# GLA block on one core: the projections' stage reordered (operand turns, token sums, gate rows, decays, r's weights)

## The chip, the core and the metric

The kernel runs on one core of one Trainium2 chip. The metric is the device time of one execution in microseconds. A core has TensorE (PE; its weight loads are PEld), VectorE (DVE), ScalarE (ACT), GpSimd (POOL) and SyncE (SP), which issues nearly all DMAs here; all of them run on their own and meet at semaphores.

## What is computed

One decoder layer on 1024 tokens of width 1024, in float32: RMSNorm, gated linear attention, residual, RMSNorm, squared-ReLU MLP, residual, and a final RMSNorm. What matters here is the head of the mixer:

```python
proj = h @ w_in
q, k, v, r, gk_low = jnp.split(proj, ...)          # 512, 512, 1024, 1024, 16 columns
log_a = jax.nn.log_sigmoid(gk_low @ w_gk_up + b_gk) / 16
...                                                 # per chunk: cumulative sum b of log_a
o_inter = einsum(q * exp(b), state); attn = (q, k, decay by differences of b); k_dec = k * exp(b_last - b)
...
o = rms_norm(o, g_onorm); return (o * silu(r)) @ w_out
```

h is the normed x. The norm's per-token factor (rstd) isn't applied to x: the projections run on x times the norm's gain, and rstd is put in where it is used.

## The kernel before

**Products.** Large products are done in a fast 2 x 2 block form with seven block products instead of eight: each side has blocks "11", "12", "21", "22" of 512 x 512, and some of the seven operands are sums of blocks, built in place ("t" is a temporary). `form` (lines 142 to 148) lists, for the n-th product, the operand and the sums that it needs first. A side of one form sums n=1: t = 21 + 22; n=2: t = t - 11 and 21 = 11 - 21; n=3: t = 12 - t; the other form has t = 12 - 11, then t = 22 - t and 12 = 22 - 12, and for the last product t = 21 - t. A block product is one *step*: 4 lanes of 128 rows by 4 slices of k, and for each three matmuls of 128x128x512, since every operand is split into a high and a low part (`split`, lines 77 to 80: ACT copies to the rounded type, DVE subtracts). So a step has 48 matmuls and takes four splits of 128x1024, two for each side. Step (i, at) is the at-th step of chunk i; its n is taken from PLAIN = (0, 5, 1, 2, 3, 4, 6). Chunk 0 is Q and K (weights W as stationary side, x as moving side), chunk 1 is V (x stationary, weights moving).

**Order.** `chunks_of` (lines 241 to 279) walks the steps: it runs the hooks of step (i, at), asks for the next weights at steps 5 and 6, makes the operands of the *next* step (`operand`: sums and splits), and then issues the matmuls of this one. A hook with four numbers (i, at, lane, kp) runs inside the step, behind that lane's matmuls of that k slice; such a step goes lane by lane. PE's instructions keep the order of the source. Those of the other engines and of SP's DMA queue are ordered by a planner: each has the place in the source as its priority, evictions (lines 422 and 437) are raised, and the planner issues what it reckons ready. On the chip each engine then follows that fixed order.

**Buffers.** SBUF tiles come from tags with few buffers: "big" 8 (split operands, four for each step), "vx" 8 (x blocks, later v), "wa" 6 and "wb" 4 (weights and "t"), "raw" 2, "g4" 6, "hq" 4. PSUM has "gl" 5 and "mm" 3. A tile is taken when one of its tag is free.

**The stage.** Lines 338 to 376 load the first blocks of x and W, then the others, w_gk (the 16 gate columns) and w_up. Lines 379 to 388 split the gate weights. `gk_half` (line 391) computes 16 gate rows for half of the tokens in 16 matmuls on x's split operands: the first half ahead of step (0,1), the second ahead of step (0,5), on an x "12" split of its own (`x12_split`, line 730). `token_rms` (line 401) squares x row by row on ACT for rstd. Each x operand of chunk 0 but n = 0 and 5 is stored to DRAM (`xv`, line 311) and read back in chunk 1 by `KeptX` (line 443), which for n = 0 and 5 fetches x again and splits it. `spread_rms` (line 467) puts rstd into the gate rows. `prep_fast` (line 505) makes one head's gates and decays for half of the tokens, four for the first half in steps (1,0) and (1,1). `load_wr` (line 677) fetches and splits r's weights, eight pieces of 512 KB. Behind chunk 1 come, for each of eight token blocks, `r_part` (line 695, 48 matmuls in four parts), the state, the outputs, and `outputs_T` (line 663), which transposes the block's output; the last block's runs in a hook of the output projection's first step.

## Time and profile before

| | us |
|---|---|
| median of 3 runs (1053.05 to 1056.13) | 1053.35 |
| profiled execution, its own time | 1055.77 |
| its span | 1054.0 |
| PE busy | 1016.8 |
| DVE busy | 730.7 |
| ACT busy | 548.2 |
| mean granted clock of TensorE | 0.986 |

The profile is of one execution. Its views name an instruction by line, engine and operation, then "out<-in" by tile names without their numbers ("big<-wa" writes a split operand from a weight tile), and how many are merged (x16). In the timeline a bracket tells how long the engine stood before and what ended that. Durations of matmuls include the tail of the pipeline, so two rows can overlap. In a table of stretches each engine has its busy time and its number of instructions; then come the granted clock of TensorE (1.00 is full speed), the mean share of the DMA engines in use, and GB/s.

### The profile page before, as it was taken

How to read it: one execution, taken by the hardware profiler on the slowest of the kernel's cores; microseconds unless marked ns; L12 is line 12 of the kernel's file. 1: busy time of each engine (PE TensorE's matmuls, PEld its weight loads, DVE VectorE, ACT ScalarE, POOL GpSimd, SP SyncE). 2: the span in 40 equal slices, each digit the busy share in tenths (PEclk: the TensorE clock that was granted, in tenths of full speed). 3: DMA queues.
4: the chain of work that ended last, by engine and by line, in shares of the span. 5: the costliest groups of instructions: out<-in, count | busy, mean ns of one | idle time of the engine just before them, and what ended most of it. 6: DMA issues, size and time to landing. Idle time of an engine off the chain costs nothing.

```text
span 1054.0 us, 12272 instructions
## 1 busy us (share of the span) xinstructions
PE 1016.8 (96%) x4614; PEld 842.8 (80%) x4614; DVE 730.7 (69%) x910; ACT 548.2 (52%) x828; POOL 198.5 (19%) x114
## 2 busy tenths in 40 slices
PE   7889889999999999999999999999999999999996
PEld 6768668778888788888888888888888888888885
DVE  5975594567657897897987336986427975338975
ACT  6571664566657436866633345533347332547355
POOL 0000030100000000004224232404330404331361
PEclk9999899999999999999999999999999999999998
DMA  9779575432224421477122575033674043762004
GB/s 267 254 307 343 199 269 211 123 105 82 92 81 154 127 71 49 181 284 275 40 81 67 205 290 217 21 91 110 219 299 160 1 121 118 274 233 94 1 1 163
DMA packets 104340, 165.33 MB, mean 157 GB/s; under 512 B 5584, under 2 KB 75344, under 8 KB 94032
## 3 DMA queue, kind: packets, MB, share of 16 engines
q1 hardware_dynamic: 104128, 164.45, 44.9%
q8 instruction: 38, 0.62, 0.2%
q14 instruction: 30, 0.25, 0.1%
q10 hardware_dynamic: 144, 0.01, 0.0%
HBM read 128.79 MB, written 35.65 MB: 156 GB/s over the span
## 4 chain that ended last, share of the span: by engine, by line
PE 87%; ACT 4%; DVE 4%; DMA 3%; issue 1%; SPq 1%; ACTq 0%; DVEq 0%
PE gl L70 52%; PE mm L70 33%; DMA raw<-in_w_r 1%; DMA wb<-in_w_head 1%; DVE big L80 1%; ACT big L79 1%; PE mm L870 1%; DVE g L502 1%; ACT g L405 1%; ACT big L324 0%; PE gl L669 0%; DMA wa<-in_w_head 0%; DVE vx L835 0%; DVE vx L439 0%; PE gl L589 0%
## 5 line engine op out<-in xcount | busy, mean ns | idle before, releaser
L70 PE MATMUL gl<-big,big 128*128 128x512 f32 x2508 | 590.7, 393 | 16.3 <-DVE big L80 8.9
L70 PEld LDWEIGHTS gl<-big,big 128*128 128x128 f32 x2508 | 473.2, 189 | 117.1 <-DVE big L80 10.8
L70 PE MATMUL mm<-big,big 128*128 128x512 f32 x1188 | 284.3, 394 | 0.0
L70 PEld LDWEIGHTS mm<-big,big 128*128 128x128 f32 x1188 | 226.3, 191 | 48.0 <-ACT g L496 0.3
L80 DVE TENSOR_TENSOR big<-wa,big 128x1024 fp32r<-128x1024 f32 (+1 forms) x112 | 152.3, 1385 | 108.7 <-ACT big L79 108.6
L79 ACT ACTIVATE big<-wa 128x1024 fp32r<-128x1024 f32 (+1 forms) x112 | 112.0, 1037 | 128.2 <-PE gl L70 58.3
L168 POOL TENSOR_TENSOR wa<-wa,wb 128x1024 f32<-128x1024 f32 x14 | 42.9, 3066 | 353.7 <-DVE big L80 353.7
L168 POOL TENSOR_TENSOR wa<-wa,wa 128x1024 f32<-128x1024 f32 x28 | 75.2, 2691 | 160.5 <-DVE big L80 159.6
L70 PE MATMUL mm<-big,wb 128*128 128x512 f32 x384 | 96.7, 400 | 4.1 <-DVE big L80 2.2
L80 DVE TENSOR_TENSOR big<-hq,big 128x1024 fp32r<-128x1024 f32 x48 | 61.4, 1282 | 45.9 <-ACT big L79 45.9
L80 DVE TENSOR_TENSOR big<-wb,big 128x1024 fp32r<-128x1024 f32 x42 | 56.4, 1354 | 48.5 <-ACT big L79 47.7
L70 PEld LDWEIGHTS mm<-big,wb 128*128 128x128 f32 x384 | 70.3, 188 | 20.5 <-DVE big L80 3.7
L79 ACT ACTIVATE big<-raw 128x1024 fp32r<-128x1024 f32 x50 | 51.9, 1056 | 62.5 <-DVE raw L168 23.9
L80 DVE TENSOR_TENSOR big<-raw,big 128x1024 fp32r<-128x1024 f32 x50 | 76.7, 1545 | 9.6 <-ACT big L79 9.6
L79 ACT ACTIVATE big<-wb 128x1024 fp32r<-128x1024 f32 x42 | 43.2, 1053 | 69.2 <-PE mm L70 42.6
L79 ACT ACTIVATE big<-hq 128x1024 fp32r<-128x1024 f32 x48 | 48.5, 1053 | 57.5 <-PE gl L70 35.9
L835 DVE TENSOR_TENSOR vx<-gl,vx 128x512 f32<-128x512 f32 x95 | 63.1, 681 | 6.9 <-PE gl L70 6.7
L510 POOL COPY top<-g 128x4 f32<-128x4 f32 x8 | 13.0, 1628 | 237.4 <-ACT g L496 130.1
L168 POOL TENSOR_TENSOR wa<-wb,wa 128x1024 f32<-128x1024 f32 x14 | 41.1, 2946 | 44.7 <-DVE big L80 44.7
L893 ACT ACTIVATE hq<-hq 128x1024 f32<-128x1024 f32 x24 | 25.4, 1058 | 29.6 <-DVE hq L886 29.6
L835 DVE TENSOR_TENSOR vx<-mm,vx 128x512 f32<-128x512 f32 x45 | 30.1, 680 | 1.7 <-PE mm L70 1.4
L70 PE MATMUL gl<-wb,wa 128*128 128x256 f32 x180 | 31.2, 304 | 0.0
(180 smaller groups left out, 803.7 us busy)
## 6 DMA issues: line engine op xcount, KB each, us to landing
big<-xw SPq DMA_DIRECT2D x42, 1024.0 KB, 6.8
xv<-big SPq DMA_DIRECT2D x14, 1024.0 KB, 5.9
xw<-big SPq DMA_DIRECT2D x14, 1024.0 KB, 5.0
big<-xv SPq DMA_DIRECT2D x10, 1024.0 KB, 6.8
wb<-xv SPq DMA_DIRECT2D x32, 256.0 KB, 3.4
wb<-in_w_ff SPq DMA_DIRECT2D x32, 256.0 KB, 3.5
wa<-in_w_ff SPq DMA_DIRECT2D x32, 256.0 KB, 3.7
wa<-in_w_ff SPq DMA_DIRECT2D x16, 512.0 KB, 4.7
```

The lines of the kernel that those rows point to most:

```text
L70: pe.matmul(o, w, m, start=start, stop=stop, skip_group_check=partial)
L79: act.activation(hi, src, AF.Copy)
L80: dve.tensor_tensor(lo, src, f32(hi), op=ALU.subtract)
L168: self.eng.tensor_tensor(*(self.ap(b, kp, 2) for b in (o, x_, y_)), op=op)
L405: act.activation(xr, xr, AF.Square, accum_out=ss1[:, t:t + 1])
L502: dve.tensor_tensor_scan(l[:, cs], ones, r[:, cs], 0.0, op0=ALU.mult, op1=ALU.add)
L510: pool.tensor_copy(top[:, 8 * h + 4 * hf:8 * h + 4 * hf + 4].unsqueeze(2), a[:, :, P - 1:P])
L835: return dve.tensor_tensor(xd, p_, xd, op=ALU.add)
L870: pe.transpose(p_[:, c * P:(c + 1) * P], xn[4 * hf + c][:, kt * P:(kt + 1) * P], ident)
L893: act.activation(d2, d2, AF.Relu)
```

## The change

- `form` can make both "late" pairs of sums (21 = 11 - 21 or 12 = 22 - 12) with n=4, which uses them, instead of n=2. All sides of chunks 0 and 1 that sum do so.
- `operand` takes its turns (x: sums of x, X: split of x, w and n: sums of W for this and the next step, W: split of W) from a list. The default is as before; for step (0,1) it is "XW" and for (0,2) "xXwWn".
- w_gk is fetched ahead of x "21"; the split of w_up moves to step (0,3); the token squares, four and four, to (0,4) and (0,5).
- `KeptX` splits n = 0 and 5 from the x blocks that are still in SBUF. For the second gate rows x "12" is fetched again at (1,2), split at (1,4) and stored; these rows are computed ahead of (1,5).
- `spread_rms` works on one half of the tokens at a time, at (1,0) and (1,5). `prep_fast` is cut in two: `gate_in` (one matmul and two activations) stays where it was, the rest of heads 0 to 3 goes to (1,1), (1,2), (1,3) and (1,4). The scan takes both of its inputs itself, so one addition goes. Head 0 of the second half moves from (1,5) to (1,6).
- r's weights: fetches and splits are apart. The first four pieces are fetched at (1,5) and the others at (1,6), six of the eight into "wa" buffers; the first four are split at (1,6), the others after chunk 1. Token block 0 takes r's parts in the order (0,0), (0,1), (1,0), (1,1) of (output half, x half).
- The last block's transposes move from lane 1 to lane 3 of the output projection's first step.

```diff
-        def form(s_form):
-
+        def form(s_form, late):
+
+
+            if late:
+                f = [list(e) for e in form(s_form, False)]
+                f[4][1], f[2][1] = f[2][1][1:], f[2][1][:1]
+                return f
...
-                out = []
                 which, order = plan[i][2], plan[i][4]
-                for w, s in enumerate(plan[i][:2]):
-                    if w != which:
-                        s.sums(order[at])
-                    out.append(s.split(order[at]))
-                    if at < 6 and w == which:
-                        s.sums(order[at + 1])
-                return out
+                w, x_ = plan[i][which], plan[i][1 - which]
+                made = {}
+                for turn in turns.get((i, at), ("W", "n", "x", "X") if which == 0 else ("x", "X", "W", "n")):
+                    if turn == "x":
+                        x_.sums(order[at])
+                    elif turn == "X":
+                        made[1 - which] = x_.split(order[at])
+                    elif turn == "w":
+                        w.sums(order[at])
+                    elif turn == "W":
+                        made[which] = w.split(order[at])
+                    elif at < 6:
+                        w.sums(order[at + 1])
+                return made[0], made[1]
...
-        wqk = weight_side(True, from_qk, dve)
+        wqk = weight_side(True, from_qk, dve, late=True)
...
-        xq = Side(False, {}, dve, pair_temp, made=lambda n, tiles: n not in (0, 5) and keep(n, tiles))
+        xq = Side(False, {}, dve, pair_temp, made=lambda n, tiles: n not in (0, 5) and keep(n, tiles), late=True)
...
+        wgu, wgs = new("g4"), new("g4", F32R)
+        wgr, wur = wgu[:, 0:128], wgu[:, 512:1024]
+        nc.sync.dma_start(wgr, w_gk)
         load_x("21")
         wqk.load("12")
-        wgu = new("g4")
-        wgr, wur = wgu[:, 0:128], wgu[:, 512:1024]
-        nc.sync.dma_start(wgr, w_gk)
...
+        def split_up():
+            act.activation(wus, wur, AF.Copy)
+            for r0 in (32, 96):
+                rs = slice(r0, r0 + 32)
+                dve.tensor_tensor(wus[rs, :], wur[rs, :], f32(wus[rs, :]), op=ALU.subtract)
+
         box = {}
...
                 for hl in range(2):
                     mm(pg, wgs[:, kt * P:(kt + 1) * P], part(kt, hl), kt == 0 and hl == 0, kt == KT - 1 and hl == 1)
-            act.activation(box["gk"][:, half(hf)], pg, AF.Copy)
-
-        def token_rms():
-            for t in range(TT):
+            return pg
+
+        def token_rms(ts):
+            for t in ts:
                 xr = new("g4")
                 nc.sync.dma_start(xr, x[t * P:(t + 1) * P, :])
                 act.activation(xr, xr, AF.Square, accum_out=ss1[:, t:t + 1])
-            rstd_of(rstd1, ss1, 8, D)
...
             def split(self, n):
-                out = [kl(new("big", F32R)) for _ in range(2)]
+                out = self.tiles[n] = [kl(new("big", F32R)) for _ in range(2)]
                 for kh in range(2):
                     if n in (0, 5):
-                        raw = new("raw")
-                        kt = 2 * kh + (4 if n == 5 else 0)
-                        nc.sync.dma_start(raw.rearrange("p (k t) -> p k t", k=2), x_piece(kt, 2, 0))
-                        for k in range(2):
-                            scaled_split(out[kh][:, k, 0, :], out[kh][:, k, 1, :], raw[:, half(k)], kt + k)
+                        split(out[kh][:, :, 0, :], out[kh][:, :, 1, :], xq.blocks["21" if n else "11"](2 * kh, 2))
                     else:
                         nc.sync.dma_start(out[kh].rearrange("p k l t -> p (k l t)").bitcast(F32), xv[n][kh])
                 if n in (0, 5):
                     keep(n, out)
                 return out
 
...
-        def spread_rms():
-
-            dg, rbc = new("g4"), new("g4")
-            for hf in range(2):
-                pb = new("mm")
-                for c in range(4):
-                    cs = slice(hf * 512 + c * P, hf * 512 + c * P + P)
-                    dve.tensor_scalar(dg[:, cs], ident, rstd1[:, hf * 4 + c:hf * 4 + c + 1], None, op0=ALU.mult)
-                    mm(pb[:, c * P:c * P + P], ones, dg[:, cs], True, True)
-                act.activation(rbc[:, half(hf)], pb, AF.Copy)
...
+        def spread_rms(hf):
+
+            u = new("g4")
+            dg, rbc = u[:, 0:512], u[:, 512:1024]
+            pb = new("mm")
+            for c in range(4):
+                cs = slice(c * P, c * P + P)
+                dve.tensor_scalar(dg[:, cs], ident, rstd1[:, hf * 4 + c:hf * 4 + c + 1], None, op0=ALU.mult)
+                mm(pb[:, cs], ones, dg[:, cs], True, True)
+            act.activation(rbc, pb, AF.Copy)
+            if hf == 0:
+                box["gk"] = new("g4", F32R)
+            raw, gk = box["raw"][hf], box["gk"][:, half(hf)]
+            dst = raw if hf == 0 else dg
+            dve.tensor_tensor(dst, raw, rbc, op=ALU.mult)
+            act.activation(gk, dst, AF.Copy)
+            dve.tensor_tensor(gk[64:128, :], dst[64:128, :], f32(gk[64:128, :]), op=ALU.subtract)
...
+            box["u", h, hf] = l, r
+
+        def gate(h, hf):
+
+            l, r = box.pop(("u", h, hf))
             act.activation(l, l, AF.Exp, scale=-1.0)
             act.activation(l, l, AF.Ln, bias=one)
-            dve.tensor_tensor(r, r, l, op=ALU.add)
             for c in range(4):
                 cs = slice(c * P, c * P + P)
-                dve.tensor_tensor_scan(l[:, cs], ones, r[:, cs], 0.0, op0=ALU.mult, op1=ALU.add)
+                dve.tensor_tensor_scan(l[:, cs], r[:, cs], l[:, cs], 0.0, op0=ALU.add, op1=ALU.add)
...
-        def prep_fast(h, hf, bank_tag):
-            a_, w = gate(h, hf, bank_tag)
+        def prep_fast(h, hf):
+            a_, w = gate(h, hf)
...
-        def load_wr(a, kq):
-            raw = new("raw")
+        def load_wr(a, kq, tag):
+            raw = new(tag)
             for k in range(2):
                 nc.sync.dma_start(raw[:, half(k)].rearrange("p (f c) -> p f c", c=P),
                                   w_r[4 * a:4 * a + 4, :, (2 * kq + k) * P:(2 * kq + k + 1) * P].rearrange("f p c -> p f c"))
+            wraw[a, kq] = raw
+
+        def split_wr(a, kq):
+            raw = wraw.pop((a, kq))
             w = kl(new("big", F32R))
             split(w[:, :, 0, :], w[:, :, 1, :], raw.rearrange("p (k f) -> p k f", k=2))
             wr[a, kq] = w
...
         def r_part(t, n):
 
-            a, i = ((0, 0), (1, 0), (1, 1), (0, 1))[n]
-            if n in (0, 1):
+            a, i = (((0, 0), (1, 0), (1, 1), (0, 1)) if t else ((0, 0), (0, 1), (1, 0), (1, 1)))[n]
+            if i == 0:
                 rbank[a] = new("mm")
             u = xt_[t, i]
             for k in range(4):
                 kt = 4 * i + k
                 w = wr[a, kt // 2][:, kt % 2]
                 mm3(rbank[a], u[:, 2 * k, :], u[:, 2 * k + 1, :], w[:, 0, :], w[:, 1, :], kt == 0, kt == 7)
-            if n == 2:
-                rr[t] = new("raw")
             if i == 1:
+                if t not in rr:
+                    rr[t] = new("raw")
...
+        def x12_load():
+            box["x12"] = [new("raw"), new("g4")]
+            for kh in range(2):
+                nc.sync.dma_start(box["x12"][kh].rearrange("p (k t) -> p k t", k=2), x_piece(2 * kh, 2, 1))
 
         def x12_split():
-            x12 = box["x12"] = [[new("g4", F32R) for hl in range(2)] for kh in range(2)]
             for kh in range(2):
+                raw, hi, lo = box["x12"][kh], new("g4", F32R), new("g4" if kh else "raw", F32R)
+                for k in range(2):
+                    scaled_split(hi[:, half(k)], lo[:, half(k)], raw[:, half(k)], 2 * kh + k)
+                box["x12"][kh] = hi, lo
...
         def gk_second():
-            gk_half(1, lambda kt, hl: box["x12"][kt // 2][hl][:, half(kt % 2)] if kt < 4
-                    else xlive[3][kt % 4 // 2][:, kt % 2, hl, :])
-
-        wv = weight_side(True, from_v, dve)
+            box["raw"].append(gk_rows(lambda kt, hl: box["x12"][kt // 2][hl][:, half(kt % 2)] if kt < 4
+                                      else xk.tiles[3][kt % 4 // 2][:, kt % 2, hl, :]))
+
...
-        hooks = {(0, 1): (gk_first,), (0, 2): (token_rms, x12_split), (0, 5): (gk_second,)}
+        hooks = {(0, 1): (gk_first,), (0, 3): (split_up,),
+                 (0, 4): (g(token_rms, range(0, 4)),), (0, 5): (g(token_rms, range(4, 8)),),
+                 (1, 0, 0, 3): (g(spread_rms, 0),),
+                 (1, 2): (x12_load,), (1, 4): (x12_split,), (1, 5): (gk_second, g(spread_rms, 1))}
...
-            hooks.update({(1, 0, 0, 3): (spread_rms,),
-                          (1, 0, 2, 3): (g(prep_fast, 0, 0, "mm"), g(prep_fast, 1, 0, "mm")),
-                          (1, 0, 3, 3): (g(prep_fast, 2, 0, "mm"),),
-                          (1, 1, 0, 1): (g(prep_fast, 3, 0, "mm"),),
-                          (1, 5, 2, 3): (g(prep_fast, 0, 1, "mm"),),
-                          (1, 6): tuple(g(load_wr, 0, kq) for kq in range(4)),
+            hooks.update({(1, 0, 2, 3): (g(gate_in, 0, 0, "mm"), g(gate_in, 1, 0, "mm")),
+                          (1, 0, 3, 3): (g(gate_in, 2, 0, "mm"),),
+                          (1, 1, 0, 1): (g(gate_in, 3, 0, "mm"), g(prep_fast, 0, 0)),
+                          (1, 2): (g(prep_fast, 1, 0), x12_load),
+                          (1, 3): (g(prep_fast, 2, 0),),
+                          (1, 4): (g(prep_fast, 3, 0), x12_split),
+                          (1, 5): (gk_second, g(spread_rms, 1)) + tuple(g(load_wr, 0, kq, "wa") for kq in range(4)),
+                          (1, 6): tuple(g(f, a, kq, *tag) for f, a, kq, tag in
+                                        [(split_wr, 0, kq, ()) for kq in range(4)]
+                                        + [(load_wr, 1, kq, ("wa" if kq > 1 else "raw",)) for kq in range(4)]),
+                          (1, 6, 2, 1): (g(gate_in, 0, 1, "mm"), g(prep_fast, 0, 1)),
                           (1, 6, 3, 1): (g(operands, 0, "mm"),)})
-        chunks_of([(wqk, xq, 0, qk_into, PLAIN), (KeptX(), wv, 1, v_into, PLAIN)], ops_a, hooks, {})
+        chunks_of([(wqk, xq, 0, qk_into, PLAIN), (xk, wv, 1, v_into, PLAIN)], ops_a, hooks, {},
+                  turns={(0, 1): "XW", (0, 2): "xXwWn"})
...
         load_xt(0, 0)
         load_xt(0, 1)
-        for kq in range(4):
-            load_wr(1, kq)
+        if not general:
+            for kq in range(4):
+                split_wr(1, kq)
...
-        hooks[0, 0, 1, 3] = (g(outputs_T, TT - 1, "mm"),)
+        hooks[0, 0, 3, 3] = (g(outputs_T, TT - 1, "mm"),)
```

More of the change, by code (lines that the diff above doesn't have):

```diff
@@ L153, in run, with __init__ @@
         class Side:
-            def __init__(self, s_form, blocks, eng, temp, made=None):
+            def __init__(self, s_form, blocks, eng, temp, made=None, late=False):
                 self.s_form, self.form, self.blocks, self.eng, self.temp, self.made = (
-                    s_form, form(s_form), blocks, eng, temp, made)
+                    s_form, form(s_form, late), blocks, eng, temp, made)
             def ap(self, name, kp, n):
@@ L191, in run, with weight_side @@
                   False: {"11": "wb", "12": "wa", "22": "wa", "21": "wb"}}
-        def weight_side(s_form, src, eng, first_tag=None):
-            side = Side(s_form, {}, eng, lambda: in_pair([new("wa"), new("wa")]))
+        def weight_side(s_form, src, eng, first_tag=None, late=False):
+            side = Side(s_form, {}, eng, lambda: in_pair([new("wa"), new("wa")]), late=late)
             def load(name):
@@ L384, in run, with gk_rows @@
         wus = new("wup", F32R)
-        act.activation(wus, wur, AF.Copy)
-        for r0 in (32, 96):
-            rs = slice(r0, r0 + 32)
-            dve.tensor_tensor(wus[rs, :], wur[rs, :], f32(wus[rs, :]), op=ALU.subtract)
+        def split_up():
[3 more added lines that the diff above has]
+                dve.tensor_tensor(wus[rs, :], wur[rs, :], f32(wus[rs, :]), op=ALU.subtract)
         box = {}
-        def gk_half(hf, part):
-            if hf == 0:
-                box["gk"] = new("g4")
+        def gk_rows(part):
             pg = new("mm")
@@ L445, in run, with __init__ @@
             s_form = False
+            def __init__(self):
+                self.tiles = {}
             def sums(self, n):
@@ L463, in split, with gate_in @@
                 return out
[L465 to L483 removed]
+        def spread_rms(hf):
[14 more added lines that the diff above has]
+            dve.tensor_tensor(gk[64:128, :], dst[64:128, :], f32(gk[64:128, :]), op=ALU.subtract)
         def chunks(ap):
             return ap.rearrange("p (c t) -> p c t", t=P)
[L489 removed]
+        def gate_in(h, hf, bank_tag):
             zp = new(bank_tag)
@@ L763, in run @@
         load_xt(0, 0)
         load_xt(0, 1)
-        for kq in range(4):
-            load_wr(1, kq)
+        if not general:
+            for kq in range(4):
+                split_wr(1, kq)
         v_split(0)
```

46 lines of the change are left out of this document (22 added, 24 removed).

## The prediction

> **What bounds the kernel now.** I read the busy shares first, then the stretches cut at step ends, then the waits and the timeline at each stretch that loses time.
>
> ```profile
> span 1054.0 us, 12272 instructions
> PE 1016.8 (96%) x4614; PEld 842.8 (80%) x4614; DVE 730.7 (69%) x910; ACT 548.2 (52%) x828; POOL 198.5 (19%) x114
> ```
>
> TensorE (PE) bounds the whole, so the change can win only where PE stands or runs at a low clock. Each of the next rows is one stretch, cut where a step ends: length, then busy time and instructions of PE, PEld, DVE, ACT and POOL, the granted clock, and DMA share and GB/s. The last row, from the chain of waits, is 54 matmuls back to back.
>
> ```profile
> 19.05:39.74 20.69, 16.43 (x65) 13.21 (x65) 17.82 (x21) 15.69 (x25) 0.00 (x0) 0.92 0.85 260
> 39.74:54.99 15.25, 12.43 (x48) 9.96 (x48) 14.47 (x14) 7.21 (x12) 0.00 (x0) 0.89 0.73 276
> 54.99:66.19 11.20, 11.20 (x50) 8.95 (x48) 7.68 (x8) 11.20 (x20) 0.00 (x0) 1.00 0.66 234
> 66.19:82.98 16.79, 13.06 (x50) 10.45 (x50) 12.95 (x19) 7.88 (x10) 0.00 (x0) 0.90 0.94 367
> 82.98:86.44 3.46, 3.46 (x17) 2.85 (x16) 3.37 (x10) 1.76 (x2) 0.00 (x0) 1.00 0.92 263
> 86.44:108.36 21.92, 21.92 (x97) 17.84 (x95) 10.14 (x11) 3.58 (x6) 0.00 (x0) 1.00 0.86 302
> 108.36:132.48 24.12, 19.58 (x82) 15.70 (x81) 13.73 (x17) 17.65 (x28) 0.00 (x0) 0.86 0.64 230
> 132.48:141.17 8.69, 8.69 (x38) 6.86 (x37) 8.66 (x19) 8.11 (x15) 2.31 (x3) 1.00 0.91 313
> 141.17:157.53 16.36, 12.43 (x48) 10.10 (x48) 15.61 (x24) 7.75 (x13) 7.15 (x4) 0.90 0.59 233
> 157.53:202.64 45.11, 45.11 (x207) 37.55 (x205) 24.76 (x32) 21.06 (x29) 5.20 (x7) 1.00 0.49 168
> 202.64:219.44 16.80, 12.66 (x50) 8.70 (x48) 7.14 (x8) 7.86 (x10) 0.00 (x0) 1.00 0.50 146
> 157.69 12.24 PE gl L70 x54
> ```
>
> A matmul at full clock costs 12.24/54 = 0.227 us, a step of 48 costs 10.88. Loss of a stretch = length less its matmuls at that price:
>
> - first gate rows (16) and step (0,1), 64 matmuls: 20.69 - 14.5 = **6.2**
> - step (0,2): 15.25 - 10.88 = **4.4**
> - step (0,4): 16.79 - 10.88 = **5.9**
> - step (1,0), where 16 of the 82 are the small ones that spread rstd (about 2.0) and two are cut at the borders, so 64 wide ones: 24.12 - 14.5 - 2.0 = **7.6**
> - step (1,2): 16.36 - 10.88 = **5.5**
> - r of token block 0: 16.80 - 10.88 = **5.9**
>
> Together **35.5 us**, clock losses included; the other stretches lose nothing. That is the most this stage can give.
>
> **The change part by part.** The timeline (start, length, engine, line) shows what each loss waits for. First the gate rows:
>
> ```profile
> 12.79 2.75 ACT L319 ACTIVATE vx<-vx,vec 128x512 f32<-128x512 f32 x4 [0.39 <-DMA vx<-in_xT]
> 14.62 0.45 SPq L370 DMA_DIRECT2D g<-in_w_gk  x1
> 19.30 1.22 DVE L80 TENSOR_TENSOR big<-wb,big 128x1024 fp32r<-128x1024 f32 x1 [6.80 <-ACT big L79]
> 21.86 1.06 ACT L79 ACTIVATE big<-vx 128x1024 fp32r<-128x1024 f32 x1
> 22.36 0.89 DVE L80 TENSOR_TENSOR g<-g,g 128x128 fp32r<-128x128 f32 x4
> 23.30 5.52 PE L70 MATMUL mm<-big,g 128*128 128x512 f32 x16 [4.26 <-DVE g L80]
> 26.57 1.22 DVE L80 TENSOR_TENSOR big<-vx,big 128x1024 fp32r<-128x1024 f32 x1
> ```
>
> w_gk is fetched behind W "12", and x "21", scaled by 15.5, isn't split before 21.9 because W's turn comes first. The edit fetches w_gk ahead of x "21" (that costs x "21" and W "12" one issue, 0.45; nothing later) and splits x first. Then ACT splits x "21" by 15.5 + 2 x 1.05 = 17.6 and DVE by 18.9, later by what evictions of step (0,0) come between; PE starts the gate rows at 19.05 and needs x "21" only in their second half, 1.8 later. The splits of the gate weights (0.89 on DVE, and taken as much on ACT) now come in step (0,0), in the 6.80 that DVE stood before 19.30; if they fall among the splits that feed step (0,0) instead, PE pays up to 1.8. Step (0,1) then waits for W "12", split next, at about 21 to 23. Left over: 1.0 of 6.2 (0 to 3).
>
> Next, steps (0,2) to (0,6):
>
> ```profile
> 40.35 1.22 DVE L168 TENSOR_TENSOR wa<-wa,wa 128x1024 f32<-128x1024 f32 x1
> 41.48 1.22 DVE L80 TENSOR_TENSOR big<-raw,big 128x1024 fp32r<-128x1024 f32 x1
> 42.75 1.49 PE L70 MATMUL gl<-big,big 128*128 128x512 f32 x5 [2.83 <-DVE big L80]
> 42.73 1.39 DVE L388 TENSOR_TENSOR wup<-g,wup 32x512 fp32r<-32x512 f32 x2
> L405 ACT ACTIVATE g<-g 128x1024 f32<-128x1024 f32 x8 | 8.4, 1050 | 0.0
> L80 DVE TENSOR_TENSOR g<-vx,g 128x1024 fp32r<-128x1024 f32 x2 | 2.5, 1225 | 3.7 <-ACT g L79 3.7
> ```
>
> A sum that only step n=4 needs (21 = 11 - 21) runs on DVE right ahead of the split PE waits for. "late" moves both such pairs on, two of 1.22 per side; the w_up split (1.39 DVE) moves to (0,3); ACT's eight token squares (8.4), which with the x "12" splits held step (0,4), go to (0,4) and (0,5), and x "12" goes into V. With the squares go eight loads of 512 KB on SP, each of which needs a buffer that a square frees: they now stand behind the stored operands of the early steps and ahead of W's loads for V, which is where a late square would be felt next. rstd, their result, is needed at (1,0), a step after the last of them. DVE is what comes due next. It worked 17.82 + 14.47 + 7.68 + 12.95 + 3.37 + 10.14 = 66.4 us from 19.05 to 108.36; less x "12" (2.5) some 64 stay. PE needs 3.63 + 6 x 10.88 = 68.9 to the end of (0,6). So DVE must be 93% busy, a little more than it reached up to 54.99 ((17.82 + 14.47)/35.94 = 90%): it just fits if nothing stands in the wrong place. I leave 4.0 of the 10.3 of steps (0,2) and (0,4) (bounds 1 and 16: nearly free flow, or DVE keeping its mean of 66.4/89.31 = 74%, so that all of QK's 16.5 stays).
>
> V's first steps:
>
> ```profile
> 97.38 0.98 SPq L456 DMA_DIRECT2D raw<-in_xT  x2
> 108.90 2.54 ACT L324 ACTIVATE big<-raw,vec 128x512 fp32r<-128x512 f32 x4
> 109.64 2.74 DVE L327 SCALAR_TENSOR_TENSOR big<-raw,vec,big 128x512 fp32r<-128x512 f32 x4 [2.56 <-ACT big L324]
> L499 DVE TENSOR_TENSOR g<-g 128x512 f32<-128x512 f32 x5 | 3.4, 679 | 2.3 <-ACT g L498 2.3
> L502 DVE TENSOR_TENSOR_SCAN g<-ones,g 128x128 f32<-128x128 f32 x20 | 7.0, 403 | 0.0
> 145.11 1.46 PE L70 MATMUL gl<-big,big 128*128 128x512 f32 x5 [3.94 <-DVE big L80]
> big<-xv SPq DMA_DIRECT2D x10, 1024.0 KB, 6.8
> ```
>
> Step (1,0) waits for x blocks fetched a second time, issued at 97.38 and only split from 108.90. After the change they are split from tiles that still lie in SBUF: four transfers of 512 KB go, and the eight half splits on ACT and DVE (2.54 and 2.74 for four) become four whole ones (1.05 and 1.22), no dearer. Step (1,2) waits 3.94 for a split on DVE, where four heads' decays stand in one place; these now come one to a step, each without its 0.68 us add (folded into the scan; the new form of scan isn't in the trace: 0.40 like the old, at worst 0.40 + 0.68/4, which only cancels the saving). Added: x "12" fetched again, split at (1,4), kept as before, and the second gate rows and rstd's second half at (1,5). PE's order is written by hand, so at (1,5) PE stands for x "12" with all of step (1,5) behind it. In step (1,4), ahead of it, DVE has a decay (scans 7.0/5 = 1.4 and three passes of 0.68), two W splits (2.4), four adds (at 0.68, 2.7) and x "12" (2.7): 11.2 against 10.88. A decay's inputs are there two steps earlier, so it can run ahead, and I leave 1.0 there, bounds 0 and 4 (the 11.2 one after another with x "12" last, and a low clock behind the gap). In (1,0) I leave 1.5 (bounds 0 and 7.6: V's weights now have to come 20 us earlier through the same queue) and in (1,2) 1.0 (0 and 3).
>
> r's weights:
>
> ```profile
> SPq L680 <- DVE big L80: 26.0, 6, 18.3
> L79 ACT ACTIVATE big<-raw 128x1024 fp32r<-128x1024 f32 x14 | 14.6, 1053 | 7.5 <-DMA raw<-in_w_r 5.9 <-PE mm L70 1.7
> ```
>
> With two raw buffers, fetch, split and fetch take turns. After, all eight pieces lie in SBUF in time; block 0 does the first output half first (24 matmuls, 5.4 us), which covers four splits (1.05 + 4 x 1.22 = 5.9). Left over: 1.0 of 5.9. That uncovers 0.5 if no other split delays it, and 3 if (1,6)'s other work does.
>
> Last, the transposes of token block 7 move two lanes later:
>
> ```profile
> 353.00 0.33 PE L669 MATMUL mm<-ident,g 128*128 128x128 f32 x1 [0.86 <-DVE g L659]
> 353.99 2.11 PE L669 MATMUL mm<-ident,g 128*128 128x128 f32 x7 [0.66 <-DVE g L659]
> 354.00:356.00 2.00, 1.87 (x8) 1.49 (x9) 0.72 (x2) 0.71 (x2) 0.00 (x0) 0.65 0.04 12
> 356.00:358.00 2.00, 2.00 (x6) 1.55 (x6) 1.84 (x2) 0.96 (x3) 0.00 (x0) 0.50 0.00 0
> ```
>
> The waits are 0.86 + 0.66 and the lower clock costs 2 x 0.35 + 2 x 0.5 = 1.7: **3.2**. Two lanes are 5.4 us of cover, and the readers of these columns come a step later, so I leave 0.3.
>
> These rows also price a short gap: the clock fell to 0.50 after waits of 0.86 and 0.66 around transposes. I charge 1.7 once for what is left over.
> [...]
>
> **Sum.** To win: 35.5 + 3.2 = 38.7. Left over: 1.0 + 4.0 + 1.5 + 1.0 + 1.0 + 1.0 + 0.3 + 1.7 = 11.5. Gain 27.2 us. The profiled execution took 1055.77 (its span 1054.0 and 1.77 around it), so it would take 1028.6; it stands 2.4 above the median of the runs, 1053.35, and against that I forecast **1026.2 us**.
>
> **Rivals.** *Fed too slowly*: DVE or DMA bounds QK. For it: DVE at 93%, and the stretches from 19.05 to 108.36 moved about 25.9 MB (length x GB/s). Without x "12"'s 2 MB kept and one x block of 1 MB read again, some 23 MB stay to be moved in 69 us: at the 367 GB/s of one stretch 63 us, at the mean of 290 GB/s 79 us, 10 too many. Against: the mean includes waits of the queue that the new order shortens. DVE at 74% leaves 11.5 us more than the 5.0 I left in QK's 16.5, less the 1.7 of the gap, DMA at its mean 10: about **1036**.
>
> *All stalls go*: only r's and a gap's remains stay, 2 to 4 us; against it speaks that same DVE share. 1053.35 - 38.7 + 3 = about **1018**.
>
> *Slower*: V's stored x operands arrive late. Each is two transfers of 1 MB that land in 6.8 us, can be issued only when PE frees the buffers, and share SP's one queue with x "12" (1 MB read, 2 MB kept) and r's weights (4 MB), all now in (1,2) to (1,6). A step covers 10.88. The change loses once each of these five operands lands more than 10.88 + 27.2/5 = 16.3 us after its buffers are free; at 17.5 it is 33 in all, 6 more than the gain: about **1059**. Against: r's weights go into buffers that free early, and steps (1,3) to (1,6) now run on a DMA share of 0.49.
>
> *It doesn't do what it says*: the order of ACT, DVE and SP is made by the planner, not by the source, so the moved work may land where it was: within 3 us of **1053**.
>
> **How the numbers follow.** Forecast 0.62 (its own range 1020 to 1031), fed too slowly 0.18, all gone 0.09, slower 0.07, not done 0.04. The range 1017 to 1042 holds the first three but for their tails. No change means within 0.3%, 3.2 us, about what a measurement of this kernel can tell. Faster 0.88, same 0.05, slower 0.07.
>
> **What would show it.** PE should pass from step (0,0) into the gate rows without the 4.26 wait; stand some 5 us in all up to (0,6); begin V at about 94 instead of 112; wait for nothing fetched from xT a second time in (1,0); and enter r's second half with no wait for w_r. Waits of PE on DVE's splits in (0,2) to (0,5) would mean the first rival, PE waiting on stored x in V the slower one. I am wrong if the gain is under 12 us, or if a wait at (1,5) eats V's part.

## The result, and the profile after

The changed kernel takes 1022.26 us (median of 4 runs, 1019.92 to 1022.41); the kernel before, beside it on the same chip, 1053.61 (4 runs, 1053.05 to 1056.13). The ratio is 0.9693, 95% interval 0.9672 to 0.9714: 31.35 us less by the medians. The forecast was 1026.2, so the gain came out 4.1 us larger than the 27.2 of the sum. The profiled execution took 1022.23 us.

The head of its page:

```profile
span 1020.5 us, 12268 instructions
PE 1004.5 (98%) x4614; PEld 837.6 (82%) x4614; DVE 723.5 (71%) x900; ACT 546.6 (54%) x825; POOL 196.9 (19%) x114
```

The span is 33.5 us shorter. PE's busy time fell by 12.3 with the same 4614 matmuls. Most of that is the clock: the mean granted clock rose from 0.986 to 0.995, which over some 1010 us of busy time is about 9 (an estimate), because a matmul takes longer at a low clock (2 us hold five at 0.59 and nine at 1.00 in rows of the last section). The other 21.2 are time in which PE stood.

The changed kernel in stretches, again cut where steps end (length, then busy time and instructions of PE, PEld, DVE, ACT and POOL, granted clock, DMA share, GB/s):

```profile
19.55:35.78 16.23, 15.46 (x66) 11.92 (x65) 13.37 (x14) 11.93 (x17) 0.00 (x0) 1.00 0.78 223
35.78:50.00 14.22, 12.38 (x48) 10.12 (x48) 14.22 (x14) 9.69 (x13) 0.00 (x0) 0.88 0.63 234
50.00:62.20 12.20, 12.20 (x55) 10.13 (x54) 12.14 (x13) 9.80 (x15) 0.00 (x0) 1.00 0.85 329
71.70:96.20 24.50, 24.50 (x111) 20.31 (x110) 15.43 (x26) 16.66 (x24) 0.00 (x0) 1.00 1.06 387
96.20:108.90 12.70, 12.70 (x61) 10.65 (x61) 7.25 (x8) 8.92 (x16) 0.00 (x0) 1.00 0.80 314
117.28:129.00 11.72, 11.06 (x49) 9.12 (x49) 11.72 (x19) 5.94 (x11) 3.47 (x3) 1.00 0.89 349
150.69:178.60 27.91, 27.91 (x135) 23.47 (x134) 15.63 (x21) 15.05 (x21) 0.19 (x1) 1.00 0.88 255
178.60:189.50 10.90, 10.90 (x50) 9.01 (x50) 7.85 (x10) 6.38 (x10) 1.08 (x1) 1.00 0.11 32
```

At 0.227 us for each wide matmul, three stretches still lose: the gate rows with step (0,1), 16.23 - 14.53 = 1.7; step (0,2), 14.22 - 10.88 = 3.3; step (1,2), 11.72 - 10.88 = 0.8. That is 5.8 of the 38.7 that could be won. (The border at 35.78 lies two matmuls inside (0,2), so some 0.4 of the 1.7 belongs to that step.) In all other rows PE is busy from end to end at full clock.

What PE waited for (total, times, longest), and its timeline at these places:

```profile
PE gl L70 <- DVE big L80: 2.5, 2, 1.8
PE gl L70 <- ACT big L79: 1.5, 1, 1.5
```

```profile
23.42 0.96 PE L70 MATMUL mm<-big,g 128*128 128x512 f32 x3 [0.77 <-DVE big L80]
...
37.62 1.81 PE L70 MATMUL gl<-big,big 128*128 128x512 f32 x4 [1.84 <-DVE big L80]
...
96.02 1.05 PE L70 MATMUL mm<-g,ones 128*128 128x128 f32 x8
...
178.44 11.06 PE L70 MATMUL mm<-big,wb 128*128 128x512 f32 x48
...
327.32 1.03 PE L683 MATMUL mm<-ident,g 128*128 128x128 f32 x8
```

The two waits of the first row are those of (0,2) and (1,2); the 1.5 on ACT lies ahead of 19.55, outside the change's reach. The 4.26 ahead of the gate rows has become 0.77 inside them; with the 1.84 of (0,2) PE stands 2.6 up to the end of (0,6), where the prediction had some 5. The small matmuls that spread rstd stand behind the first lane of (1,0), 12 matmuls of 0.227; so V begins at 96.02 - 2.7 = 93.3, against the 94 forecast. All 48 matmuls of r in block 0 run in one piece, and so do the transposes of block 7. PE's list of waits names no DMA, so V's stored operands, which it reads as they land, are never late.

DVE just ahead of the wait in (0,2):

```profile
31.93 1.22 DVE L173 TENSOR_TENSOR wa<-wa,wa 128x1024 f32<-128x1024 f32 x1
...
36.35 1.22 DVE L80 TENSOR_TENSOR big<-wa,big 128x1024 fp32r<-128x1024 f32 x1
```

The first row (one unit of 21 = 11 - 21) is one of the sums that the source now makes "late"; the planner has put it early all the same. The split that PE waits for is the last row.

### The profile page after: what moved, and what is told of

It is laid out like the page before. It is cut to its first block, busy times and chain, and to the rows that moved or that the text cites. A ratio compares the mean times of both kernels' runs of the same rounds, so it can differ in the third digit from the quotient of the medians.

```text
span 1020.5 us, 12268 instructions
## 1 busy us (share of the span) xinstructions
PE 1004.5 (98%) x4614; PEld 837.6 (82%) x4614; DVE 723.5 (71%) x900; ACT 546.6 (54%) x825; POOL 196.9 (19%) x114
## 4 chain that ended last, share of the span: by engine, by line
PE 93%; DMA 2%; DVE 2%; SPq 1%; issue 1%; ACT 1%; ACTq 0%; DVEq 0%
PE gl L70 57%; PE mm L70 35%; DMA wb<-in_w_head 1%; PE mm L911 1%; PE gl L683 1%; SPq L300 0%; DVE big L80 0%; DMA wa<-in_w_head 0%; DMA g<-in_w_up 0%; PE gl L603 0%; DVE vx L876 0%; DVE g L901 0%; ACT g L981 0%; ACT st L982 0%; SPq L345 0%
## 5 line engine op out<-in xcount | busy, mean ns | idle before, releaser
L70 PE MATMUL mm<-big,big 128*128 128x512 f32 x1188 | 280.8, 391 | 0.0
L80 DVE TENSOR_TENSOR big<-wa,big 128x1024 fp32r<-128x1024 f32 (+1 forms) x118 | 159.6, 1379 | 105.0 <-ACT big L79 105.0
L79 ACT ACTIVATE big<-wa 128x1024 fp32r<-128x1024 f32 (+1 forms) x118 | 118.2, 1038 | 133.0 <-PE gl L70 62.6
L79 ACT ACTIVATE big<-hq 128x1024 fp32r<-128x1024 f32 x48 | 48.5, 1053 | 54.0 <-PE gl L70 32.5
L79 ACT ACTIVATE big<-raw 128x1024 fp32r<-128x1024 f32 x44 | 45.6, 1058 | 55.8 <-DVE raw L173 27.6
L79 ACT ACTIVATE big<-wb 128x1024 fp32r<-128x1024 f32 x42 | 43.0, 1052 | 57.4 <-PE mm L70 30.8
L80 DVE TENSOR_TENSOR big<-raw,big 128x1024 fp32r<-128x1024 f32 x44 | 69.1, 1590 | 2.5 <-ACT big L79 2.5
L523 POOL COPY top<-g 128x4 f32<-128x4 f32 x8 | 5.1, 635 | 206.3 <-DVE g L515 206.3
```

Source lines behind the costliest of these rows:

```text
L70: pe.matmul(o, w, m, start=start, stop=stop, skip_group_check=partial)
L79: act.activation(hi, src, AF.Copy)
L80: dve.tensor_tensor(lo, src, f32(hi), op=ALU.subtract)
L523: pool.tensor_copy(top[:, 8 * h + 4 * hf:8 * h + 4 * hf + 4].unsqueeze(2), a[:, :, P - 1:P])
```

## The experiments

Each kernel below is the changed kernel with one edit, timed against the kernel before on one chip. The distance to the changed kernel is the difference of the two ratios times 1054 us. With intervals of 0.0016 and 0.0021 on them such a distance is known to about 2.8 us, so smaller ones are read from the traces and called so.

### The turns of (0,1) and (0,2)

```diff
-                  turns={(0, 1): "XW", (0, 2): "xXwWn"})
+        )
```

> The changed kernel, but steps (0,1) and (0,2) take their operands in the old order (W and its next sums ahead of x). Theory (each wait belongs to one edit, and its undoing brings that wait back): PE waits for x 21 ahead of the gate rows again, some 3 to 4 us with the low clock behind it, and (0,2) keeps its own wait of 1.8: about 1026 to 1028. Rival (the planner orders ACT and DVE by what it reckons ready, the turns in the source hardly matter): within 1 us of 1022.3. Rival (DVE bounds the whole of QK, so a wait moved early only takes the place of a later one): within 1 us, with the wait of (0,2) gone.

Measured: 1030.12 us, ratio 0.9763 (0.9747 to 0.9779), 7.4 us more. What PE waited for (total, times, longest); the rows with "mm" are the gate rows:

```profile
PE gl L70 <- DVE big L80: 3.2, 1, 3.2
PE mm L70 <- ACT big L79: 2.2, 2, 1.7
PE mm L70 <- DVE big L80: 2.0, 2, 1.1
```

In the gate rows PE waits 2.2 + 2.0 = 4.2 in all for the splits of x, against 0.77 in the changed kernel. (Before the change it stood 4.26 there, put down to the split of the gate weights, whose earlier fetch stays in this run.) The wait of (0,2) grows from 1.84 to 3.2. The order in the source does reach ACT and DVE here, and most of this stretch's gain hangs on it. The expectation, 1026 to 1028, was too low: it left (0,2) at 1.8. Both turns were undone at once, so which of them lengthens (0,2) was not separated.

### The late sums

```diff
-        wqk = weight_side(True, from_qk, dve, late=True)
+        wqk = weight_side(True, from_qk, dve, late=False)
```

and the same for x in QK and for V's weights.

> The changed kernel, but no side makes sums late: 21 = 11 - 21 and 12 = 22 - 12 stand with n=2 as before. Theory (the sum in front of the split is what held step (0,2)): two more sums of 1.22 us of DVE ahead of the split of (0,2), 2.4 us, and a low clock of 1 to 2 behind the longer gap: 1025 to 1027. Rival (the planner had put one of W's two sums early anyway, and the others fall where DVE has slack): 1022 to 1023.5. In V no wait comes back by either.

Measured: 1025.18 us, ratio 0.9713 (0.9697 to 0.9729), 2.1 more, within the uncertainty. That is the time the first theory forecast, but the trace puts it elsewhere:

```profile
37.62 1.30 PE L70 MATMUL gl<-big,big 128*128 128x512 f32 x4 [1.84 <-DVE big L80]
...
52.37 13.85 PE L70 MATMUL gl<-big,big 128*128 128x512 f32 x53 [2.21 <-DVE big L80]
```

The wait of (0,2) is the same 1.84, and a new one of 2.21 stands a step later, in (0,3). The sums do cost PE time, but not where the first theory (and the prediction) had them.

### The token squares, x "12", and both

The squares in one place:

```diff
-                 (0, 4): (g(token_rms, range(0, 4)),), (0, 5): (g(token_rms, range(4, 8)),),
+        hooks = {(0, 1): (gk_first,), (0, 2): (g(token_rms, range(8)),), (0, 3): (split_up,),
```

> The changed kernel, but all eight token squares with their eight loads stand at step (0,2) again; x 12 stays in V and the split of w_up at (0,3). Theory (the squares hold ACT, and with it the splits that (0,3) and (0,4) wait for): 8.4 us of ACT in one place, and half a MB per load ahead of the operands, bring 3 to 6 us of waits back in (0,3) or (0,4): 1025 to 1028. Rival (the squares only hurt together with the splits of x 12, which are gone from here): within 1 us of 1022.3.

x "12" in QK:

```diff
+                split(h3, l3, xq.blocks["12"](2 * kh, 2))
...
+        hooks = {(0, 1): (gk_first,), (0, 2): (x12_split,), (0, 3): (split_up,),
+                 (0, 4): (g(token_rms, range(0, 4)),), (0, 5): (g(token_rms, range(4, 8)), gk_second),
```

> The changed kernel, but x 12 is split in QK at step (0,2) from the block that lies in SBUF, kept to DRAM there, and the second gate rows are computed at (0,5); the squares stay spread over (0,4) and (0,5). Theory (QK is just fed: DVE at 93 per cent needed, so 2.5 us more of DVE, 2 of ACT and 2 MB of stores come out as PE waits): 1025 to 1028, the waits in (0,3) to (0,5). Rival (QK has slack left: PE never waits from (0,3) to (1,1) in the changed kernel): within 1 us, or up to 1 us less since V has 1 MB less to read.

Both, as before the change:

```diff
+        hooks = {(0, 1): (gk_first,), (0, 2): (g(token_rms, range(8)), x12_split), (0, 3): (split_up,),
+                 (0, 5): (gk_second,),
```

> The changed kernel, but both the eight token squares and the split and store of x 12 stand at step (0,2) again, the second gate rows at (0,5). One at a time they moved the time by -1 (squares) and +5 (x 12, with its loss in (1,2), not in QK). Theory (step (0,4)'s wait of before, 3.7 us and a low clock, needs both in one place): 3 to 6 us in (0,3) or (0,4) beside those 5: 1030 to 1034. Rival (QK's new order of the operands absorbs both): 1026 to 1028, no wait over 1 us in (0,3) to (0,6).

Measured: the squares alone 1021.25 us, 0.9680 (0.9664 to 0.9696), 1.4 less, which is no difference; x "12" alone 1027.55, 0.9740 (0.9721 to 0.9758), 5.0 more; both 1026.75, 0.9729 (0.9714 to 0.9744), 3.8 more. For the squares, alone and together with x "12", the rivals hold and not the theories. PE with x "12" in QK, then DVE and ACT of the same kernel ahead of the long wait:

```profile
48.49 12.31 PE L70 MATMUL gl<-big,big 128*128 128x512 f32 x53 [0.38 <-DVE big L80]
...
122.11 0.77 PE L70 MATMUL gl<-big,big 128*128 128x512 f32 x1 [2.80 <-ACT big L79]
```

```profile
120.13 0.73 DVE L515 TENSOR_TENSOR_SCAN g<-g 128x128 f32<-128x128 f32 x2
...
120.90 0.21 ACT L522 ACTIVATE est<-g 128x4 f32<-128x4 f32 x1 [1.45 <-DVE g L515]
...
121.01 1.99 ACT L79 ACTIVATE big<-wa 128x1024 fp32r<-128x1024 f32 x2
...
122.08 2.36 DVE L80 TENSOR_TENSOR big<-wa,big 128x1024 fp32r<-128x1024 f32 x2
```

QK takes the 2.5 us more of DVE and the 2 MB of stores with no wait over 0.4 behind (0,2). What is lost is lost in (1,2), where PE stands 2.80 for W's high part and 0.49 more for its low part, against 0.66 in the changed kernel. ACT comes to W's split (L79) only at 121.01, behind a decay's activation (L522) that stood 1.45 for DVE's scan (L515). In the changed kernel it does so at 114.44, though step (1,1) begins only 2.25 earlier there (108.73 instead of 110.98). V has less work here than in the changed kernel, so what costs is the order that the planner made of it; why it made this one the record doesn't show. As far as the trace shows, the 5.0 are thus not the price of x "12" in QK. With both moved back it is the same picture, a wait of 1.14 on ACT and this one in (1,2):

```profile
122.22 2.50 PE L70 MATMUL gl<-big,big 128*128 128x512 f32 x5 [2.35 <-DVE big L80]
```

So neither the squares nor x "12" nor the two together bring step (0,4)'s old loss of 5.9 back while the other edits stand. Undoing the turns, or the late sums, brought no wait there either. Which combination had made that wait is open: the pair was not put back together with the old turns or the early sums.

### V's second fetch of x

```diff
-                        split(out[kh][:, :, 0, :], out[kh][:, :, 1, :], xq.blocks["21" if n else "11"](2 * kh, 2))
+                        raw = new("raw")
+                        kt = 2 * kh + (4 if n == 5 else 0)
+                        nc.sync.dma_start(raw.rearrange("p (k t) -> p k t", k=2), x_piece(kt, 2, 0))
+                        for k in range(2):
+                            scaled_split(out[kh][:, k, 0, :], out[kh][:, k, 1, :], raw[:, half(k)], kt + k)
```

> The changed kernel, but V's operands n=0 and n=5 are made from x fetched again (four transfers of 512 KB, half splits) as before. Theory (in step (1,0) PE waited for this second fetch): a wait of 3 to 4 us ahead of (1,0), with a low clock behind it: 1026 to 1029. Rival (the fetch came late only because QK itself was late in its queue; now it lies hidden): within 1 us of 1022.3.

Measured: 1031.47 us, ratio 0.9778 (0.9762 to 0.9794), 9.0 more. The timeline of SP's queue, ACT and PE:

```profile
87.64 1.12 SPq L471 DMA_DIRECT2D raw<-in_xT  x2
...
94.25 2.63 ACT L335 ACTIVATE big<-raw,vec 128x512 fp32r<-128x512 f32 x4 [2.73 <-DMA raw<-in_xT]
96.79 1.99 ACT L79 ACTIVATE big<-wa 128x1024 fp32r<-128x1024 f32 x2
...
97.88 0.79 PE L70 MATMUL gl<-big,big 128*128 128x512 f32 x1 [6.99 <-ACT big L79]
```

The fetch is issued 6.6 us before its first use, and ACT, which follows a fixed order, takes V's weights only behind it; so PE waits 6.99, and the wait is put down to the weights' split; 1.52 more on DVE's part of that split follow. The cause is the fetch, though the wait names another tile. The theory had the cause right and the size too small, 3 to 4.

### The decays, alone and with the second fetch

```diff
-                          (1, 1, 0, 1): (g(gate_in, 3, 0, "mm"), g(prep_fast, 0, 0)),
-                          (1, 2): (g(prep_fast, 1, 0), x12_load),
-                          (1, 3): (g(prep_fast, 2, 0),),
-                          (1, 4): (g(prep_fast, 3, 0), x12_split),
+            hooks.update({(1, 0, 2, 3): (g(gate_in, 0, 0, "mm"), g(prep_fast, 0, 0), g(gate_in, 1, 0, "mm"), g(prep_fast, 1, 0)),
+                          (1, 0, 3, 3): (g(gate_in, 2, 0, "mm"), g(prep_fast, 2, 0)),
+                          (1, 1, 0, 1): (g(gate_in, 3, 0, "mm"), g(prep_fast, 3, 0)),
```

> The changed kernel, but the decays of heads 0 to 3 stand right behind their gate inputs again, in steps (1,0) and (1,1); the scan stays the new one. Theory (four decays in one place hold DVE ahead of the split that (1,2) waits for): the wait of 3.9 us in (1,2) comes back as 3 to 4.5 us with its low clock: 1025.5 to 1027. Rival (the missing add of 0.68 per head and the x operands that need no half splits any more leave DVE room enough): within 1 us.

Then the same with the second fetch of x and with the old scan:

```diff
+            dve.tensor_tensor(r, r, l, op=ALU.add)
-                dve.tensor_tensor_scan(l[:, cs], r[:, cs], l[:, cs], 0.0, op0=ALU.add, op1=ALU.add)
+                dve.tensor_tensor_scan(l[:, cs], ones, r[:, cs], 0.0, op0=ALU.mult, op1=ALU.add)
```

> The changed kernel, but V's first steps as before in three things at once: x for n=0 and n=5 fetched again and split in halves, the four decays in one place, and the add ahead of the scan. By the sum of the two undone one at a time (9.0 and 0.6) it is 1032. Theory (the 3.9 us wait of (1,2) came from DVE's load of half splits and decays together, neither alone): that wait is back, 4 to 5.5 more: 1035.5 to 1038. Rival (that wait came from QK ending late): none in (1,2), 1031 to 1033.

Measured: the decays alone 1023.24 us, 0.9699 (0.9683 to 0.9715), 0.6 more, no difference; all three 1038.32, 0.9835 (0.9820 to 0.9850), 15.0 more, which is 6.0 beyond the second fetch alone. PE in (1,2), first of the one and then of the other:

```profile
116.20 1.42 PE L70 MATMUL gl<-big,big 128*128 128x512 f32 x5 [0.91 <-DVE big L80]
```

```profile
132.20 2.41 PE L70 MATMUL gl<-big,big 128*128 128x512 f32 x5 [4.19 <-DVE big L80]
```

The first scan on DVE, again of the one and of the other:

```profile
103.65 1.37 DVE L515 TENSOR_TENSOR_SCAN g<-g 128x128 f32<-128x128 f32 x4 [2.36 <-ACT g L512]
```

```profile
120.34 1.37 DVE L520 TENSOR_TENSOR_SCAN g<-ones,g 128x128 f32<-128x128 f32 x4
```

The wait of 3.94 that the kernel before had in (1,2) is there again, at 4.19, only when the second fetch, the gathered decays and the add stand together. The theory had DVE loaded by half splits and decays at once, but the half splits end at 113.7, and DVE stands 2.25 before it comes to the decays. What the rows show is the time at which the decays begin. With the decays alone the first scan comes 2.6 ahead of step (1,1), which begins at 106.22; with all three it comes 1.0 behind its begin at 119.33, since ACT makes the late x operand and a split of W before the first gate inputs. DVE then works without a gap, on decays and V's evictions, up to W's split for (1,2) at 130.94. Spreading the decays is worth nothing once x is not fetched again. How much of the 4.19 is the add (four of 0.68) was not separated.

### r's weights

```diff
-                          (1, 5): (gk_second, g(spread_rms, 1)) + tuple(g(load_wr, 0, kq, "wa") for kq in range(4)),
+                          (1, 5): (gk_second, g(spread_rms, 1)),
-                                        [(split_wr, 0, kq, ()) for kq in range(4)]
-                                        + [(load_wr, 1, kq, ("wa" if kq > 1 else "raw",)) for kq in range(4)]),
+                                        [(f, 0, kq, tag) for kq in range(4)
+                                         for f, tag in ((load_wr, ("raw",)), (split_wr, ()))]),
...
+                load_wr(1, kq, "raw")
```

and the old order of r's parts in block 0.

> The changed kernel, but r's weights are fetched and split through the two raw buffers again, piece by piece, the first four at (1,6) and the others behind chunk 1, and block 0 takes r's parts in the old order. Theory (fetch, split, fetch take turns on two buffers, PE waits for them in r of block 0): 4 to 6 us with the low clock: 1026 to 1028.5. Rival (the queue is free earlier now, so the pieces land in time): within 1 us.

Measured: 1026.81 us, ratio 0.9732 (0.9716 to 0.9748), 4.1 more. PE in r:

```profile
183.61 1.66 PE L70 MATMUL mm<-big,wb 128*128 128x512 f32 x6 [0.55 <-DVE big L80]
186.01 1.43 PE L70 MATMUL mm<-big,wb 128*128 128x512 f32 x5 [0.74 <-DVE big L80]
188.44 0.50 PE L70 MATMUL mm<-big,wb 128*128 128x512 f32 x1 [1.00 <-ACT big L79]
189.70 4.17 PE L70 MATMUL mm<-big,wb 128*128 128x512 f32 x17 [0.76 <-DVE big L80]
```

Fetch, split and fetch take turns again (ACT stands 2.42 and 2.63 for pieces of w_r), and PE stands for the splits, 3.1 in these four rows: the theory holds. The two buffers and the old order of r's parts came back together, so their shares were not separated.

### The transposes

```diff
-        hooks[0, 0, 3, 3] = (g(outputs_T, TT - 1, "mm"),)
+        hooks[0, 0, 1, 3] = (g(outputs_T, TT - 1, "mm"),)
```

> The changed kernel, but the last block's transposes stand at lane 1 of the output projection's first step again. Theory: the two waits of 0.86 and 0.66 come back, and the low clock behind them: 1.5 by the waits alone, 3.2 with the clock: 1024 to 1025.5. Rival (the clock was low there for another reason): 1023.8 at most, the clock at 1.00 in that stretch.

Measured: 1024.63 us, ratio 0.9707 (0.9691 to 0.9723), 1.5 more, within the uncertainty. In the trace, PE and then the stretches behind it:

```profile
321.88 0.33 PE L683 MATMUL mm<-ident,g 128*128 128x128 f32 x1 [0.67 <-DVE g L673]
322.87 1.55 PE L683 MATMUL mm<-ident,g 128*128 128x128 f32 x7 [0.66 <-DVE g L673]
```

```profile
324.00:326.00 2.00, 2.00 (x9) 1.61 (x8) 1.11 (x1) 1.57 (x4) 0.00 (x0) 0.60 0.01 3
326.00:328.00 2.00, 2.00 (x7) 1.58 (x6) 2.00 (x3) 0.00 (x0) 0.00 (x0) 0.55 0.00 0
```

Both waits are back and the low clock with them: 0.67 + 0.66 + 2 x 0.40 + 2 x 0.45 = 3.0 in this execution, against the 3.2 that the prediction had for it. The low clock follows these two short waits in both profiles that have them, here (0.60 and 0.55) and before the change (0.65 and 0.50).

### Two attempts at what is left in (0,2)

W's late sums on GpSimd:

```diff
+                eng = self.on4 if n == 4 and self.on4 else self.eng
...
+        wqk.on4 = pool
```

> The changed kernel, but W's two late sums in QK (21 = 11 - 21) run on GpSimd, which does nothing in QK, instead of VectorE. Theory (step (0,2) is held by DVE, which is busy without a gap from 34 to 50 us, and one of these sums stands ahead of the split that PE waits for): the split comes 1.2 to 2.4 us earlier, the wait of 1.84 falls under 0.6, and the low clock that sometimes follows it stays away: 1.5 to 3 us less than the changed kernel, 1019 to 1021. Rival (the wait is set by the evictions that DVE must make first, for which it waits for PE's lanes): no gain, 1022. Rival (GpSimd takes 2.7 to 3.1 us for such a sum and DVE is slower beside it): DVE's operations of 1.22 us get longer, no gain or a loss.

Measured: 1026.24 us, ratio 0.9709 (0.9695 to 0.9722), 1.7 more, so no gain. DVE, POOL and PE:

```profile
33.26 1.76 DVE L175 TENSOR_TENSOR wa<-wa,wb 128x1024 f32<-128x1024 f32 x1
...
35.55 3.01 DVE L80 TENSOR_TENSOR big<-wa,big 128x1024 fp32r<-128x1024 f32 x1
```

```profile
31.53 2.41 POOL L175 TENSOR_TENSOR wa<-wa,wa 128x1024 f32<-128x1024 f32 x1 [26.90 <-DMA vx<-in_xT]
35.11 2.37 POOL L175 TENSOR_TENSOR wa<-wa,wa 128x1024 f32<-128x1024 f32 x1 [1.16 <-DVE wa L175]
```

```profile
38.62 2.08 PE L70 MATMUL gl<-big,big 128*128 128x512 f32 x4 [2.82 <-DVE big L80]
```

The split stands earlier in DVE's order, as wished, but takes 3.01 instead of 1.22. POOL's sum runs from 35.11 to 37.48, the split from 35.55 to 38.56, 1.08 behind POOL's end; the sum at 33.26 likewise ends 1.08 behind POOL's first, which ends at 33.94. In these rows DVE worked as if it stood until POOL was done; why, they don't show. PE's wait grew from 1.84 to 2.82. In (1,2) it grew too, from 0.66 to 1.14 on ACT and 0.78 on DVE, so the loss is not of (0,2) alone.

W's split raised in the planner:

```diff
-                        made[which] = w.split(order[at])
+                        if (i, at) in raised:
+                            with tc.high_priority():
+                                made[which] = w.split(order[at])
...
+                   turns={(0, 1): "XW", (0, 2): "xXwWn"}, raised=((0, 2),))
```

> The changed kernel, but the split of W for step (0,2) is raised in the planner, so that it stands ahead of one eviction in DVE's order; no work is taken away. Theory (an order of DVE is what holds (0,2)): the wait of 1.84 falls to about 1, 1 to 2 us less: 1020 to 1021.5. Rival (DVE has no slack from 34 to 50 us, so what comes earlier makes something else come later): the wait moves to (0,3), within 1 us of 1022.3.

Measured: 1021.70 us, ratio 0.9677 (0.9664 to 0.9690), 1.7 less. The intervals of this and of the changed kernel overlap, so it isn't shown to be better. PE:

```profile
46.21 12.35 PE L70 MATMUL gl<-big,big 128*128 128x512 f32 x53 [1.00 <-DVE big L80]
```

The wait of (0,2) is gone and one of 1.00 stands in (0,3). Theory and rival hold in part: the order made the wait larger than it need be, and DVE, which in the changed kernel is busy for all 14.22 us of the stretch 35.78 to 50.00, has no room to make it vanish. Here too (1,2) has longer waits, 1.14 and 0.78.

## Why the prediction was right, point by point

**The bound, and the ceiling of 38.7.** Right. The new profile leaves 5.8 of it, so 32.9 are won; the spans differ by 33.5. Undone by the experiments, turns 7.4, late sums 2.1, x "12" 5.0, V's first steps (three edits together) 15.0, r's weights 4.1 and transposes 1.5 make 35.1. With 2.8 us on each that is consistent with the gain but no proof of it, and the 5.0 with x "12" are paid in (1,2) for an order of the planner. The earlier fetch of w_gk and the move of w_up's split were not undone alone.

**Gate rows and (0,1): 1.0 left of 6.2.** Mechanism right (turns undone: the waits return), size 1.7.

**(0,2) and (0,4): 4.0 left of 10.3.** Measured 3.3, all in (0,2): 1.84 of wait and 14.22 - 10.88 - 1.84 = 1.5 of low clock. The number is near, in part by luck, for two steps behind it failed. That the sum 21 = 11 - 21 is what holds (0,2): of its two units one is still early, and with the sums early the wait is no longer than without; moving them spares (0,3). That the squares with x "12" held (0,4): put back together they bring no wait there. What did hold (0,4) stays open.

**"DVE must be 93% busy, it just fits".** True of the first part, not of the whole. From 19.55 to 62.20 DVE works 13.37 + 14.22 + 12.14 = 39.7 of 42.65 us, 93%, and there lies all that QK still loses. From 71.70 to 96.20 it is 15.43 of 24.50, 63%, and PE never stands. The "fed too slowly" rival has its share in (0,2), where PE waits for a split on a DVE that never stands, though a raised split shows that part of that wait is order. Behind (0,2) it has none: x "12" added to QK brought no wait over 0.4, and DMA ran at 387 GB/s beside a PE that never stood.

**(1,0): 1.5 left of 7.6.** Nothing is left, and the second fetch put back costs 9.0. Right in the cause. V's weights, which the prediction feared would come late, did not.

**(1,2): 1.0 left of 5.5.** Measured 0.8. The step that failed is its cause: "four heads' decays stand in one place" is not enough. With x split from SBUF they are done early enough even so (0.6 us, no difference); the wait of 4.19 took the second fetch beside them, which makes them begin behind the start of (1,1), and the add.

**The risk at (1,5), 1.0, r, 1.0, and the transposes, 0.3.** All came out at nothing: the stretches 150.69 to 178.60 and 178.60 to 189.50 have PE busy throughout, and the transposes have no wait. The sums of 11.2 against 10.88 in (1,4) and of 5.9 against 5.4 in r were right to warn, but the work ran ahead of its turn: x "12" was split by 139.1 and its gate rows came at 150.5; r's first four pieces were split by 169.6 and r began at 178.4.

**1.7 for a low clock behind a gap, charged once.** Measured 1.5, behind the 1.84 of (0,2); behind the 0.77 of the gate rows and the 0.66 of (1,2) the clock stayed at 1.00. That the charge fell due is luck: most profiles with the same 1.84 don't pay it (last section).

**Why 4 us more came than forecast.** By the terms, what is left fell from 11.5 to 5.8: (0,2) and (0,4) with the charge for the clock from 4.0 + 1.7 to 3.3, (1,0) from 1.5, (1,5) and r from 1.0 each and the transposes from 0.3 to nothing, (1,2) from 1.0 to 0.8, while the gate rows rose from 1.0 to 1.7. The mis-sized terms are thus the allowances for steps that turned out to run free. The profiled executions differ by 1055.77 - 1022.23 = 33.5, that is 6.3 more than the sum of 27.2. The medians show 4.1 of these, since the profile before stood 2.2 above its median and the one after at it.

**The rivals.** "All stalls go" (1018) fails on DVE in (0,2). The slower one fails on V's stored operands, for which PE waits nowhere. "It doesn't do what it says" is seen in half of one sum.

## What to carry to other kernels

The loss of each step, read off a profile as length less matmuls, forecast this change well; the causes named for the losses did worse, and two of them (the squares, the gathered decays) cost nothing that could be measured when put back alone. Before work is spread out, ask what else stands at that place in the same engine's fixed order, and try each alone and together. Follow a wait back through what the releasing engine did before, and compare start times: an order that a planner makes can shift a loss to a step that the edit never touched. An idle second engine is no free helper: look first at how long its operations make those beside them (here a DVE split took 3.01 us beside a GpSimd sum, and 1.22 without).
